# Four of 22 channel pairs of an up projection by seven products of halves, and weight sums by adding transfers

## The chip, the cores and the metric

The kernel runs on one core of one Trainium2 chip. The metric is the device time of one execution in microseconds (us). Five engines work side by side, each through its own queue in order: PE (matmuls), DVE (VectorE), ACT (ScalarE), POOL (GpSimd) and SP, which issues transfers (DMAs). On-chip memory is SBUF (128 partitions) and PSUM, where matmuls accumulate; PSUM is used here as banks of 128 x 512 f32.

## The reference, cut to what matters

One encoder block over 512 tokens of 1024 channels. The change concerns the channel mixer at its end:

```python
h2 = rmsnorm(x, norm2_w[l])
u = dwconv_centered(h2 @ ffn_up[l], ffn_conv_w[l], ffn_conv_b[l])   # 1024 -> 2 x 2816, width 3 over tokens
gate, val = jnp.split(u, 2, axis=-1)
x = x + (jax.nn.silu(gate) * val) @ ffn_down[l]                     # 2816 -> 1024
return rmsnorm(x, final_norm_w)
```

Everything is float32. The kernel keeps that precision by splitting each operand into a high part (rounded to the PE's reduced format, fp32r) and a low part (the rest), and by three matmuls for each product: high x high, high x low, low x high (`mm3`, L370 to L373).

## The kernel before

**The up projection** (534 to 776 us). The 5632 columns of ffn_up are taken as 22 channel pairs: for pair c the 128 gate columns c and the 128 value columns c. Each of the 44 jobs (`job`) loads a weight tile wr_up of 128 x 8 x 128, ACT copies it to the high part wh_up, POOL subtracts to get the low part wl_up in two operations of 512 elements a partition, and PE makes 8 x 3 matmuls over all 512 tokens into one PSUM bank, ps_up. The rings of buffers set how far ahead this may run: three wr, two wh, two wl, three banks of the ring "pp". Then `conv3` applies the width-3 convolution from PSUM: ACT makes the centre tap with the bias (L1674), DVE the two side taps (L1680), each reading the bank and adding into an SBUF tile c3. ACT applies SiLU to the gate, and DVE multiplies gate by value into a (L1701). The first job (c = 0) is done in two halves of 256 tokens.

**The down product** already uses seven products of halves instead of eight: it is cut into halves of tokens, of its 22 inner blocks (11 and 11) and of output columns (one step of the Strassen scheme, in Winograd's form). Its left operands (sums and differences of a's blocks, cut into high and low parts "as" by L1630 on ACT and L1634 on DVE) are partly made in the up stage: parts 1 and 7 for each c below 11, L1643's combinations for each c from 11. Its right operands are four sums of blocks of ffn_down. `t_unit` makes them in the up stage, eleven times: SP loads two row blocks of ffn_down into the tile tp (L1657), POOL makes four differences in place (L1665), and SP writes each to DRAM, t_scr (L1667). The down product reads them back as wr_dn.

**What sets the order.** A small list scheduler, `Planner`, holds every operation with its engine, an assumed cost, the names it reads and writes, and a key; it fixes one order for each engine before the program runs. Keys come in three ranks, FEED (weights) before EVICT (emptying PSUM) before the rest, and within a rank by the unit's number u. On the chip each engine goes through its list in order and waits only for what an instruction needs.

## Time and profile before

| | |
|---|---|
| runs of the kernel before | 891.85, 890.25, 890.43 us; median 890.43 |
| the profiled execution | 890.88 us, of which the span is 889.2 us |
| PE's mean granted clock | 0.996 of full |
| PE's busy share of the span | 98% |
| up projection on PE | first matmul 534.6 us, last 776.1 us |
| down product and final norm | to 889.2 us |

Times in rows of the profile are microseconds from the span's start, unless marked ns. A row of the groups gives line, engine, operation, tiles written <- read, shape, count | busy us, mean ns of one | idle time of the engine just before, and what ended it. A tile's or a line's row gives min/median/max ns and the first and the last start. PEld is the loading of weights into PE, which overlaps matmuls.

### The profile page before, as it was taken

To read this page: it belongs to the slowest core of one execution; us is meant where nothing else is said; L and a number is where in the kernel's file an instruction comes from. 1 tells how busy PE (TensorE), PEld (TensorE's weight loads), DVE (VectorE), ACT (ScalarE), POOL (GpSimd) and SP (SyncE) were. 2 spreads that over 40 slices of the span, in tenths; PEclk is the share of its full clock that TensorE was granted. 3 is DMA by queue.
4 is the path that set the end of the run, shared out by engine and by line. 5 is a ranking of instruction groups with operands and counts; after the bars stand their busy time and mean duration, and the time that the engine had idled before them with its cause. 6 is when DMAs were issued, how large, how long until landed. Compare 5 with 4: busy or idle time off the path is not lost.

```text
span 889.2 us, 14088 instructions
## 1 busy us (share of the span) xinstructions
PE 874.7 (98%) x5178; PEld 737.1 (83%) x5178; DVE 549.0 (62%) x980; ACT 461.0 (52%) x791; POOL 497.9 (56%) x447
## 2 busy tenths in 40 slices
PE   8999999999999999999999999999999999999996
PEld 7888888798878887988788888888888888888885
DVE  4757685357795976554434244656655554569995
ACT  6689533418868334335854334444443333456664
POOL 3444555125455553253668706778787764567663
PEclk9999999999999999999999999999999999999999
DMA  7365449324255376112898606567666753266553
GB/s 207 99 204 131 130 118 188 86 60 119 64 163 154 108 168 107 31 60 73 275 306 270 190 1 231 187 213 225 233 202 203 244 173 101 97 211 181 186 178 133
DMA packets 176265, 140.20 MB, mean 158 GB/s; under 512 B 32110, under 2 KB 143547, under 8 KB 176196
## 3 DMA queue, kind: packets, MB, share of 16 engines
q1 hardware_dynamic: 167300, 137.20, 51.1%
q10 hardware_dynamic: 8896, 2.10, 1.6%
q8 instruction: 41, 0.67, 0.3%
q14 instruction: 28, 0.23, 0.1%
HBM read 114.08 MB, written 25.20 MB: 157 GB/s over the span
## 4 chain that ended last, share of the span: by engine, by line
PE 92%; DVE 3%; ACT 2%; DMA 2%; issue 1%; SPq 0%; DVEq 0%; ACTq 0%
PE ps_up L372 9%; PE ps_up L371 9%; PE ps_up L373 9%; PE dn L373 3%; PE dn L371 3%; PE dn L372 3%; PE ps_k L371 2%; PE pw L1139 2%; PE o L1176 2%; PE ps_k L373 2%; PE ps_gp L371 2%; PE ps_k L372 2%; PE ps_wo L373 2%; PE ps_wo L372 2%; PE ps_wo L371 2%; PE ps_gp L372 2%
## 5 line engine op out<-in xcount | busy, mean ns | idle before, releaser
L396 POOL TENSOR_TENSOR wl_up<-wr_up,wh_up 128x512 fp32r<-128x512 f32 x88 | 115.2, 1330 | 50.1 <-ACT wh_up L392 47.9
L372 PE MATMUL ps_up<-h_lo,wh_up 128*128 128x512 f32 (+1 forms) x368 | 139.9, 380 | 0.3 <-DVE h_lo L541 0.3
L371 PE MATMUL ps_up<-h_hi,wh_up 128*128 128x512 f32 (+1 forms) x368 | 140.0, 380 | 0.0
L373 PE MATMUL ps_up<-h_hi,wl_up 128*128 128x512 f32 (+1 forms) x368 | 139.8, 380 | 0.0
L1680 DVE SCALAR_TENSOR_TENSOR c<-ps_up,fw,c 128x511 f32<-128x511 f32 x88 | 66.0, 750 | 99.3 <-ACT c L1674 97.5
L1665 POOL TENSOR_TENSOR tp<-tp 128x512 f32<-128x512 f32 x44 | 59.9, 1362 | 43.4 <-DMA tp<-in_ffn_down_dram 38.5
L1868 POOL TENSOR_TENSOR w_dn<-wr_dn,w_dn 128x512 fp32r<-128x512 f32 x44 | 65.6, 1504 | 29.0 <-ACT w_dn L1865 27.5
L372 PEld LDWEIGHTS ps_up<-h_lo,wh_up 128*128 128x128 f32 x368 | 69.1, 188 | 13.5 <-DVE h_lo L541 0.5
L371 PEld LDWEIGHTS ps_up<-h_hi,wh_up 128*128 128x128 f32 x368 | 69.1, 188 | 13.3
L373 PEld LDWEIGHTS ps_up<-h_hi,wl_up 128*128 128x128 f32 x368 | 69.1, 188 | 13.2
L392 ACT CAST wh_up<-wr_up 128x1024 fp32r<-128x1024 f32 x44 | 46.2, 1051 | 62.1 <-issue 22.3
L1865 ACT CAST w_dn<-wr_dn 128x512 fp32r<-128x512 f32 x69 | 42.4, 621 | 29.5 <-PE dn L373 21.1
L372 PE MATMUL dn<-w_dn,as 128*128 128x512 f32 x141 | 54.2, 385 | 0.0
L371 PE MATMUL dn<-w_dn,as 128*128 128x512 f32 x141 | 54.2, 384 | 0.0
L373 PE MATMUL dn<-w_dn,as 128*128 128x512 f32 x141 | 54.2, 384 | 0.0
L1634 DVE TENSOR_TENSOR as<-a,as 128x512 fp32r<-128x512 f32 (+1 forms) x41 | 41.8, 1044 | 0.1
L1630 ACT CAST as<-a 128x512 fp32r<-128x512 f32 (+1 forms) x41 | 21.5, 534 | 32.5 <-DVE a L1701 28.9
L396 POOL TENSOR_TENSOR wl_k<-wr_k,wh_k 128x512 fp32r<-128x512 f32 x16 | 20.3, 1288 | 31.6 <-ACT wh_k L392 22.4
L396 POOL TENSOR_TENSOR wl_v<-wr_v,wh_v 128x512 fp32r<-128x512 f32 x16 | 20.4, 1294 | 27.5 <-ACT wh_v L392 27.5
L1674 ACT ACTIVATE c<-ps_up,fw 128x512 f32<-128x512 f32 x44 | 33.9, 770 | 0.0
L396 POOL TENSOR_TENSOR wl_z<-wr_z,wh_z 128x512 fp32r<-128x512 f32 x16 | 20.3, 1292 | 23.5 <-ACT wh_z L392 19.9
L396 POOL TENSOR_TENSOR wl_gp<-wr_gp,wh_gp 128x512 fp32r<-128x512 f32 x16 | 21.5, 1360 | 19.6 <-ACT wh_gp L392 18.0
(361 smaller groups left out, 2435.8 us busy)
## 6 DMA issues: line engine op xcount, KB each, us to landing
wr_up<-in_ffn_up_dram SPq DMA_DIRECT2D x44, 512.0 KB, 3.9
tp<-in_ffn_down_dram SPq DMA_DIRECT2D x22, 512.0 KB, 5.3
t_scr<-tp SPq DMA_DIRECT2D x44, 256.0 KB, 2.5
wr_dn<-t_scr SPq DMA_DIRECT2D x20, 512.0 KB, 3.8
wr_dn<-in_ffn_down_dram SPq DMA_DIRECT2D x15, 512.0 KB, 3.6
x<-in_x_dram SPq DMA_DIRECT2D x8, 512.0 KB, 6.1
wr_k<-in_w_in_dram SPq DMA_DIRECT2D x8, 512.0 KB, 5.9
wr_z<-in_w_in_dram SPq DMA_DIRECT2D x8, 512.0 KB, 3.9
```

The costliest lines, as they stand in the source:

```text
L371: pe.matmul(ps, ahi, bhi, start=first, stop=False)
L372: pe.matmul(ps, ahi, blo, start=False, stop=False)
L373: pe.matmul(ps, alo, bhi, start=False, stop=last)
L392: act.copy(b["hi"], b["raw"])
L396: pool.tensor_tensor(out=b["lo"][:, sl], in0=b["raw"][:, sl], in1=f32(b["hi"][:, sl]), op=ALU.subtract)
L1630: act.copy(sets[p][:, i : i + n, 0, :], src())
L1634: dve.tensor_tensor(out=w[:, :, 1, :], in0=src(), in1=f32(w[:, :, 0, :]), op=ALU.subtract)
L1665: G(cp(512), lambda o=o, x=x, y=y: pool.tensor_tensor(out=w(*o), in0=w(*x), in1=w(*y), op=ALU.subtract), r=[n(*x), n(*y)], w=[n(*o)], key=u)
L1674: act.activation(b[j], box["ps"], AF.Identity, scale=fw[:, 1, ci : ci + 1], bias=fw[:, 3, ci : ci + 1])
L1680: dve.scalar_tensor_tensor(out=y[:, lo:hi], in0=box["ps"][:, lo + sh : hi + sh], scalar=fw[:, k, ci : ci + 1], in1=y[:, lo:hi], op0=ALU.mu ...
L1865: act.copy(b["w"][:, 0, :], raw["t"][:, j, :])
L1868: eng.tensor_tensor(out=b["w"][:, 1, :], in0=raw["t"][:, j, :], in1=f32(b["w"][:, 0, :]), op=ALU.subtract)
```

## The change

It has two parts and what follows from them.

**Seven products for pairs 3, 5, 7 and 9** (`SEVEN`). For such a pair the product of [gate columns | value columns] with h2 is cut into halves of the 1024 input channels (1, 2) and halves of the tokens; the two column blocks are the second cut of the weight. Seven products of 4 x 3 matmuls with 256 columns take the place of two of 8 x 3 with 512. Four sums of h2's quarters are made once (`h_sums`, into the tile h_raw) and cut into high and low parts (as_x0, as_x1). Each pair's weights need four sums of weight halves, two on POOL and two on DVE, and seven splits (wq): high parts on ACT, low parts five in seven on POOL and two on DVE. The seven PSUM results are combined on DVE into an SBUF tile u of 128 x 1024 by one copy on ACT and seven additions, and the convolution reads u in place of PSUM.

**The four weight sums of the down product** are made without SBUF: `right_sums` issues, from POOL's queue, a transfer of up to 4 x 128 rows from ffn_down (or from a finished t_scr) to t_scr, and then a transfer that adds a second block to it. There are 12 such twos, 24 transfers, spread over pairs 1 to 17. Since they add where POOL subtracted, the signs of some blocks change: the left combinations and five of the additions into the residual are subtractions now.

As the buffers of the ring "as" hold h2's sums until pair 9, parts 1 and 7 of the down product's left operands are made later, two blocks at a time, from pair 9 on (`left_early`, `left_sums`).

The core of the diff:

```diff
-        "r4": 4, "nm": 1, "x4": 3, "qe": 4, "ext": 1, "x1": 1, "x2": 1, "xs": 2, "pw": 1, "pwr": 1, "cv3": 4, "sq2": 1, "as": 2, "tp": 1, "dhl": 3,
+        "r4": 4, "nm": 1, "x4": 3, "qe": 4, "ext": 1, "x1": 1, "x2": 1, "xs": 2, "pw": 1, "pwr": 1, "cv3": 4, "sq2": 1, "as": 2, "tp": 2, "dhl": 3,
+    SEVEN = (3, 5, 7, 9)
+    VLO = (0, 3)
+    MINUS = ((0, 1, 1), (1, 1, 1), (1, 1, 7), (0, 1, 6), (1, 1, 6))
-    def t_unit(i, u):
...
+    def right_sums(j, k0, n, key, after):
...
+        first, second = {0: ((0, 0), (0, 1)), 1: (0, (1, 1)), 2: ((0, 1), (1, 1)), 3: (1, (1, 0))}[j]
+        kept = isinstance(first, int)
+        move = lambda src, **kw: pool.dma_start(flat_(j), src, **kw)
+        add("pool", 1.2, lambda: move(flat_(first) if kept else block(*first)), name(first) if kept else [], name(j),
+            key, None, 256.0 * n, after=after, land=12.0)
+        add("pool", 1.2, lambda: move(block(*second), accum_op=ALU.add), [], name(j), key, None, 256.0 * n, land=12.0)
-    def conv3(box, pp, ci, b, j, u):
+    def conv3(src, srcn, ci, b, j, u):
...
-                out=y[:, lo:hi], in0=box["ps"][:, lo + sh : hi + sh], scalar=fw[:, k, ci : ci + 1],
+                out=y[:, lo:hi], in0=src()[:, lo + sh : hi + sh], scalar=fw[:, k, ci : ci + 1],
+    def h_sums(u):
...
+        for i, o in enumerate(((0, 0), (0, 1), (1, 1), (1, 0))):
+            part(i, *o)
+        comb(4, (0, 0), (0, 0), (0, 1), ALU.subtract)
+        comb(5, (0, 1), (0, 1), (1, 1), ALU.subtract)
+        comb(6, (1, 1), (1, 1), (0, 0), ALU.add)
+        comb(7, (1, 0), (1, 0), (1, 1), ALU.subtract)
+        for i, o in enumerate(((0, 0), (1, 1), (0, 1), (1, 0))):
+            keep(i, o)
+    def seven_weights(c, u):
...
+        split(a11, k)
+        split(a12, k + 1)
+        plus(q1, a21, a22, QV[0], k + 2)
+        plus(q2, q1, a11, QV[1], k + 3)
+        split(q2, k + 4)
+        plus(a21, a21, a11, QV[2], k + 5)
+        split(a21, k + 6)
+        split(q1, k + 7)
+        plus(a12, a12, q2, QV[3], k + 8)
+        split(a12, k + 9)
+        split(a22, k + 10)
+    def seven_up(c, b):
...
+        for i in range(7):
+            tag = ("ds", "pp")[turns["l"] % 2]
...
+                mm3(p["ps"], wt_[:, 0, k, :], wt_[:, 1, k, :], *xs[i][0](k), k == 0, k == 3)
...
+            act.copy(at(1, 0), box[0][0]["ps"])
+        step((0, 0), 1, (1, 0), ALU.add)
+        step((1, 1), 2, (1, 0), ALU.subtract)
+        step((1, 0), 3, (1, 1), ALU.add)
+        step((0, 1), 4, (1, 1), ALU.subtract)
+        step((1, 1), 4, (1, 0), ALU.subtract, swap=True)
+        step((0, 1), 5, (0, 1), ALU.add)
+        step((1, 0), 6, (1, 0), ALU.add)
+    TURNS = {n: 1 for n in (1, 2, 4, 5, 7, 8, 10, 11, 13, 14, 16, 17)}
+    QV = (0, 1, 0, 1)
+    SLOTS = ("dhl", "whi", "wlo", "dhl", "whi", "wlo", "dhl")
+        if c in SEVEN:
+            u = seven_up(c, b)
+        if pos == 0:
+            h_sums(u + 1000)
+        for _ in range(TURNS.get(pos, 0)):
+            right_sums(*turn_.pop(0), 5000, [f"cv3:{c}"])
-        if c % 2 == 0:
-            t_unit(c // 2, u + 60)
```

What this does to the order is seen at three places. Names in the rows: c3_N is the convolution's tile of chunk N (gate chunks 0 to 21, value chunks 22 + c), ps_upC_J the PSUM result J of pair C, wr_uJ_C and wq_C_I the raw and the split weights of a seven-product pair, u_C its combined result; numbers at a name's end only tell buffers apart.

Place one, DVE, from the moment at which h2 is complete. Before:

```order
L1680 SCALAR_TENSOR_TENSOR c3_0_5538<-ps_up0_0_5408,fw_130,c3_0_5538 128x511 x2
L1680 SCALAR_TENSOR_TENSOR c3_22_5566<-ps_up0_1_5448,fw_130,c3_22_5566 128x511 x2
L1701 TENSOR_TENSOR a_0_5591<-c3_0_5538,c3_22_5566 128x512
L1643 TENSOR_TENSOR c3_22_5566<-a_0_5591 128x256
L1634 TENSOR_TENSOR as_1_5599<-a_0_5591,as_1_5599 128x256
L1634 TENSOR_TENSOR as_7_5604<-c3_22_5566,as_7_5604 128x256
L1680 SCALAR_TENSOR_TENSOR c3_1_5620<-ps_up1_0_5561,fw_130,c3_1_5620 128x511 x2
```

And now:

```order
L1704 TENSOR_TENSOR h_raw_5491<-h2_hi_4724,h2_lo_4725 128x4x256 x3
L1680 SCALAR_TENSOR_TENSOR c3_0_5531<-ps_up0_0_5408,fw_130,c3_0_5531 128x511 x2
L1704 TENSOR_TENSOR h_raw_5491<-h2_hi_4724,h2_lo_4725 128x4x256
L1680 SCALAR_TENSOR_TENSOR c3_22_5557<-ps_up0_1_5445,fw_130,c3_22_5557 128x511 x2
L1904 TENSOR_TENSOR a_0_5583<-c3_0_5531,c3_22_5557 128x512
L1711 TENSOR_TENSOR h_raw_5491<-h_raw_5491 128x4x256 x3
L1680 SCALAR_TENSOR_TENSOR c3_1_5603<-ps_up1_0_5552,fw_130,c3_1_5603 128x511 x2
L1711 TENSOR_TENSOR h_raw_5491<-h_raw_5491 128x4x256
```

Seven passes over quarters of h2, 1024 elements each, have come between the taps, with an eighth behind pair 1's first; the three operations on the left operands are gone from here.

Place two, DVE, what follows up to the additions of pair 3. Before, behind pair 1's product:

```order
L1643 TENSOR_TENSOR c3_23_5661<-a_0_5591 128x256
L1634 TENSOR_TENSOR as_1_5599<-a_0_5591,as_1_5599 128x256
L1634 TENSOR_TENSOR as_7_5604<-c3_23_5661,as_7_5604 128x256
L1680 SCALAR_TENSOR_TENSOR c3_2_5707<-ps_up2_0_5651,fw_130,c3_2_5707 128x511 x2
L1680 SCALAR_TENSOR_TENSOR c3_24_5747<-ps_up2_1_5696,fw_130,c3_24_5747 128x511 x2
```

And now:

```order
L1726 TENSOR_TENSOR as_x0_5610<-h_raw_5491,as_x0_5610 128x4x256 x2
L1680 SCALAR_TENSOR_TENSOR c3_23_5653<-ps_up1_1_5592,fw_130,c3_23_5653 128x511 x2
L1904 TENSOR_TENSOR a_0_5583<-c3_1_5603,c3_23_5653 128x512
L1760 TENSOR_TENSOR h_raw_5491<-h_raw_5491,wr_u0_3_5581 128x512
L1726 TENSOR_TENSOR as_x1_5634<-h_raw_5491,as_x1_5634 128x4x256
L1781 TENSOR_TENSOR wq_3_2_5699<-h_raw_5491,wq_3_2_5699 128x512
L1760 TENSOR_TENSOR wr_u0_3_5581<-wr_u0_3_5581,h_raw_5491 128x512
L1781 TENSOR_TENSOR wq_3_6_5710<-wr_u1_3_5631,wq_3_6_5710 128x512
L1680 SCALAR_TENSOR_TENSOR c3_2_5692<-ps_up2_0_5639,fw_130,c3_2_5692 128x511 x2
L1726 TENSOR_TENSOR as_x1_5634<-h_raw_5491,as_x1_5634 128x4x256
L1680 SCALAR_TENSOR_TENSOR c3_24_5747<-ps_up2_1_5681,fw_130,c3_24_5747 128x511 x2
L1840 TENSOR_TENSOR u_3_5760<-ps_up3_1_5749,u_3_5760 128x256
```

The taps of pair 2 (c3_2, c3_24), which empty its two banks, stand behind the low parts of h2's sums and behind pair 3's weights.

Place three, POOL, from pair 2's gate weights on. Before:

```order
L396 TENSOR_TENSOR wl_up2_0_5614<-wr_up2_0_5238,wh_up2_0_5613 128x512 x2
L1665 TENSOR_TENSOR tp_1_5555<-tp_1_5555 128x512
L396 TENSOR_TENSOR wl_up2_1_5656<-wr_up2_1_5572,wh_up2_1_5655 128x512 x2
L396 TENSOR_TENSOR wl_up3_0_5701<-wr_up3_0_5593,wh_up3_0_5700 128x512 x2
L1665 TENSOR_TENSOR tp_2_5688<-tp_2_5688 128x512 x2
L396 TENSOR_TENSOR wl_up3_1_5740<-wr_up3_1_5649,wh_up3_1_5739 128x512 x2
```

And now:

```order
L400 TENSOR_TENSOR wl_up2_0_5597<-wr_up2_0_5238,wh_up2_0_5596 128x512 x2
L1781 TENSOR_TENSOR wq_3_0_5619<-wr_u0_3_5581,wq_3_0_5619 128x512
L400 TENSOR_TENSOR wl_up2_1_5644<-wr_up2_1_5563,wh_up2_1_5643 128x512 x2
L1760 TENSOR_TENSOR h_raw_5491<-wr_u1_3_5631 128x512
L1760 TENSOR_TENSOR wr_u1_3_5631<-wr_u1_3_5631,wr_u0_3_5581 128x512
L1781 TENSOR_TENSOR wq_3_1_5685<-wr_u0_3_5581,wq_3_1_5685 128x512
L1664 DMA t_scr_104<-in_ffn_down_dram 512x512
L1781 TENSOR_TENSOR wq_3_3_5704<-wr_u1_3_5631,wq_3_3_5704 128x512
L1781 TENSOR_TENSOR wq_3_4_5729<-h_raw_5491,wq_3_4_5729 128x512
L1781 TENSOR_TENSOR wq_3_5_5740<-wr_u0_3_5581,wq_3_5_5740 128x512
L400 TENSOR_TENSOR wl_up4_0_5789<-wr_up4_0_5674,wh_up4_0_5788 128x512 x2
L1664 DMA t_scr_104<-in_ffn_down_dram 512x512
```

The differences in tp have gone from POOL; pair 3 brings five low parts and two sums in place of four low parts, and between them stands the first of the 24 transfers; the second follows pair 4's gate weights.

200 lines of the change are left out of this document (158 added, 42 removed).

## The prediction, made before the changed kernel ran

> **What bounds the kernel now.** First the head of the page: the span, the busy time of the engines, PE in 40 slices, and the chain of work that ended last.
>
> ```profile
> span 889.2 us, 14088 instructions
> PE 874.7 (98%) x5178; PEld 737.1 (83%) x5178; DVE 549.0 (62%) x980; ACT 461.0 (52%) x791; POOL 497.9 (56%) x447
> PE   8999999999999999999999999999999999999996
> PE 92%; DVE 3%; ACT 2%; DMA 2%; issue 1%; SPq 0%; DVEq 0%; ACTq 0%
> ```
>
> PE is full in all but the first and the last slice and holds 92% of the chain, so the time is what PE is given to do plus whatever it waits for. The second view sums PE's waits; the third is the stretch from the second pair of the up projection to the down product (busy us of each engine with the number of instructions, clock, DMA share, GB/s); the fourth, all instructions on the up projection's PSUM tile (min/median/max ns, first and last start).
>
> ```profile
> PE ps_up L372 <- DVE h_lo L541: 0.3, 1, 0.3
> ...
> 547.00:777.00 230.00, 230.00 (x1020) 190.53 (x1019) 130.84 (x163) 98.09 (x135) 167.13 (x127) 1.00 0.59 192
> ...
> L371 PE MATMUL ps_up<-h_hi,wh_up x368: 280/389/403, 534.6 to 775.6; 128*128 128x512 f32 x168, 128*128 128x256 f32 x16
> L373 PE MATMUL ps_up<-h_hi,wl_up x368: 278/389/397, 534.8 to 776.1; 128*128 128x512 f32 x168, 128*128 128x256 f32 x16
> ```
>
> In the up projection PE waits once, 0.3 us, at its start; after 547 us it is busy for all 230 us, while POOL has 167 and DVE 131. A matmul taken off PE here is worth its full step; a wait put on PE costs its full length.
>
> **The step of a matmul.** A row's 389 ns overlaps the next instruction, so the price is the distance between starts.
>
> ```profile
> 543.06 0.28 PE L371 MATMUL ps_up<-h_hi,wh_up 128*128 128x256 f32 x1
> ...
> 547.62 0.28 PE L373 MATMUL ps_up<-h_hi,wl_up 128*128 128x256 f32 x1
> 547.74 0.40 PE L371 MATMUL ps_up<-h_hi,wh_up 128*128 128x512 f32 x1
> ...
> L371 PEld LDWEIGHTS ps_up<-h_hi,wh_up 128*128 128x128 f32 x368 | 69.1, 188 | 13.3
> ```
>
> Between the first two rows lie 38 steps of a 256-column matmul: 4.56 us, 0.120 us each. From 547.74 to the last start at 776.1 lie 1007 steps of 512 columns (42 products of 24): 0.2268 us each. The half-width step is therefore 53% of the full one, not 50%. That the 188 ns of a weight load would set the pace of half-width matmuls (84 x 0.188 = 15.8 us a pair, slower) is refuted by the same rows, which load a new weight for each.
>
> **PE's gain.** A pair is now 2 x 8 x 3 = 48 steps of 512: 10.89 us. By seven products it is 7 x 4 x 3 = 84 steps of 256: 10.08 us. The gain is 0.81 us a pair, **3.24 us** for four. The down product keeps its seven products and its matmuls; only its additions into the residual change sign and operand order.
>
> **What the other engines get.** POOL loses 44 subtractions and 16 low parts (four pairs), and gets 20 low parts and 8 sums of halves of the same size, and 24 transfers to issue. DVE gets 12 passes over a quarter of h2, 8 sums, 8 low parts, and 28 additions out of PSUM. ACT gets 32 copies of small tiles for 8 of larger ones; it is busy 98 of 230 us and I count it as hidden. Their prices:
>
> ```profile
> L396 POOL TENSOR_TENSOR wl_up<-wr_up,wh_up x84: 1283/1294/1815, 546.1 to 767.8; 128x512 fp32r<-128x512 f32 x84
> L1665 POOL TENSOR_TENSOR tp<-tp x40: 1283/1296/1742, 551.5 to 717.9; 128x512 f32<-128x512 f32 x40
> L1680 DVE SCALAR_TENSOR_TENSOR c<-ps_up,fw,c x88: 737/750/753, 546.8 to 779.0; 128x511 f32<-128x511 f32 x88
> L1634 DVE TENSOR_TENSOR as<-a,as x11: 410/426/1521, 554.7 to 662.2; 128x256 fp32r<-128x256 f32 x11
> L1701 DVE TENSOR_TENSOR a<-c,c x22: 691/888/1845, 551.6 to 779.7; 128x512 f32<-128x512 f32 x22
> L522 DVE SCALAR_TENSOR_TENSOR sq<-x,nst_b,n2b 128x1024 f32<-128x1024 f32 x4 | 5.1, 1286 | 0.1
> ```
>
> POOL's account falls: 60 operations go, 28 come, so 32 x 1.295 = 41 us less, against 24 issues whose length no row shows; over the stage that is room, not gain, since PE does not wait for POOL now. DVE's grows: a pass over 1024 elements is about 1.25 us (0.41 at 256, 0.69 at 512, so 0.28 per further 256; 1.286 is the nearest row), 12 of them 15 us; 16 x 0.69 = 11 us; 28 additions of 256 elements at about 0.42 = 12 us. These 38 us would take DVE from 131 to 169 of 230 us: enough on the average. What decides is where it is needed at once, and that is ahead of the first of the four pairs.
>
> **DVE and POOL shut each other out.** In the two rows of DVE and the one of POOL (three operations), DVE's 256-element operation, 0.41 us when alone, takes 1.40 and 1.52 us beside POOL's.
>
> ```profile
> 553.37 1.40 DVE L1643 TENSOR_TENSOR c<-a 128x256 f32<-128x256 f32 x1
> 554.70 1.52 DVE L1634 TENSOR_TENSOR as<-a,as 128x256 fp32r<-128x256 f32 x1
> ...
> 551.50 4.43 POOL L1665 TENSOR_TENSOR tp<-tp 128x512 f32<-128x512 f32 x3
> ```
>
> L1680, with one input in PSUM, never does (737 to 753 ns in 88). The Trainium skill, page "SBUF — State Buffer", section "Who interferes with whom", has the rule: a DVE instruction with two SBUF inputs contends with a GpSimd instruction that reads SBUF, one with at most one does not. By that rule the trace agrees, and the 16 taps of the four pairs, which now read SBUF, fall under it too.
>
> The groups of DVE from 547 to 777 us give the mean of such a wait (mean ns is the second number):
>
> ```profile
> L1701 DVE TENSOR_TENSOR a<-c,c 128x512 f32<-128x512 f32 x21 | 21.2, 1010 | 1.1 <-ACT c L1703 0.4
> ...
> L1634 DVE TENSOR_TENSOR as<-a,as 128x256 fp32r<-128x256 f32 x11 | 10.1, 919 | 0.1
> ...
> L1634 DVE TENSOR_TENSOR as<-c,as 128x256 fp32r<-128x256 f32 x11 | 7.8, 705 | 0.7 <-ACT as L1630 0.4
> ```
>
> Over the shortest ones (691, 410, 410) that is 0.32, 0.51 and 0.30 us: 0.4 an operation.
>
> **The first seven-product pair.** h2 is complete when DVE's two h_lo operations end:
>
> ```profile
> 541.26 1.29 DVE L541 TENSOR_TENSOR h_lo<-pt_b,h_hi 128x512 fp32r<-128x512 f32 x2 [2.72 <-ACT h_hi L537]
> ```
>
> at 542.55. Pair 3 starts on PE after 96 steps from 547.74, at 569.5. Its fourth product (36 steps of 0.120 later, 573.8) takes the PSUM bank of pair 2's gate, since the ring "pp" has three; so pair 2's two taps on that bank must be done by then. By DVE's order (places one and two) there stand before their end: 11 passes of 1024 (13.8 us), 10 taps (7.5), 2 products gate x value (0.89 each, 1.8), 4 operations of 512 (2.8): 25.9 us, up to 568.4 if nothing waits. That leaves 5.4 us for the waits of 17 operations with two SBUF inputs. At 0.4 each they are 6.8 and PE stands 1.4 us. The upper end: POOL has 14 operations (18 us) in these 31, and where both engines queue they alternate, as in the rows at 551 to 556, so that most of the 17 wait up to 1.0 us; going through the two orders in turn I find some 8.5 us of waits and a stop of 3.1; ten waits of 1.0 would give 4.6. The lower end is none, if the operations fall into POOL's gaps. I take the middle of 1.4 and 3.1, **2.3 us**. The next three pairs need no passes over h2: their DVE work ahead of a product is two sums and two low parts, their weights are read a pair ahead, and I count them at nothing; if that cover is gone, it is the second rival. An addition out of PSUM is on the path only if late; 28 of them are priced above.
>
> **The transfers.** 24 issues stand in POOL's queue between low parts that PE needs, and an adding one waits there for the copy it adds to. Nearest rows:
>
> ```profile
> tp<-in_ffn_down_dram SPq DMA_DIRECT2D x22, 512.0 KB, 5.3
> wr_dn<-t_scr SPq DMA_DIRECT2D x20, 512.0 KB, 3.8
> ```
>
> A transfer of 1 MB, DRAM to DRAM, is at least 3.8 us and, at twice the slower row, 10.6; with a second operand to read up to twice that, 21. Each issue may cost POOL from nothing to about one operation (1.3 us). Between a copy and its adding transfer POOL's order leaves about 9 us at the tightest place: the second copy stands behind pair 4's gate weights, about 11 us into pair 3, its adding transfer behind pair 5's sums, about 20 us in (pair 4's gate product frees their slot at 15.5, then three POOL operations). Elsewhere it is 13 to 18. Behind the tightest one some 4 us are left until PE needs the next low part. I take 7 us, by the row it is nearest to (the load of the same data), and no cost. SP loses 66 DMAs and POOL-dependent waits; nothing waited for them but POOL.
>
> **Sum.** The profiled execution took 890.88 us: 890.88 - 3.24 + 2.3 = 889.94. It lies 0.45 above the median of the runs shown, 890.43, so against that **889.5 us**, 0.1% faster, with 888.1 to 891.7 as this case's own range (a stop of 0.9 to 4.5). The measurement tells about 0.2% (1.8 us) from no change.
>
> **Rivals.** *Nothing stops* (0.35): the passes over h2 fit the gaps, PE stays full, 890.43 - 3.24 = 887.2. For it: 5.4 us of room. Against: POOL fills 17.4 of 21 us in that stretch now, and more afterwards.
> *DVE and POOL are full in pairs 5, 7 and 9 too* (0.13): over two pairs (10.89 + 10.08 = 21.0 us of PE) POOL has 11 operations, 14.2 us, and DVE 10 with two SBUF inputs, 7.5 us (two products, four of 512, four taps): 21.7 us that exclude each other. It decides where handing over between the two saves nothing. Against: at 551 to 556 us POOL's three and two of DVE's (0.69 and 0.41 alone) took 4.43 us and not 5.0, so a hand-over saves 0.2 to 0.3. If it saves nothing, each of the three pairs is late by 1 to 1.5 us: 889.5 + 3.7 = **893.2**, slower.
> *POOL is held by an adding transfer* (0.12): it decides from a landing over 13 us; at 18 us the tightest place loses 5: **894.5**. The Trainium skill, page "Collectives: The Full Stack", section "The bandwidth ceiling: the fold count and why AG ≠ RS ≠ AR", says that a reducing transfer reads two sources and ran at about half a copy's rate there (1.93). No run here shows it; by it 7 us would be about 13, just at that point.
>
> ```profile
> 547.00:568.00 21.00, 21.00 (x98) 17.47 (x97) 14.42 (x18) 11.22 (x16) 17.43 (x14) 1.00 0.72 236
> ```
>
> **How the numbers follow.** Forecast 0.40, rivals 0.35, 0.13, 0.12. Faster by over 0.2% (below 888.65) is the first rival and the low edge of the forecast: 0.38. Within 0.2%: 0.37. Slower (above 892.2): 0.25. The range 886.8 to 893.6 holds the forecast, the first rival with 0.4 us below, and most of the second; it leaves out the third.
>
> **What would show it.** Right: PE's rows step 0.120 us through pairs 3, 5, 7 and 9, and one gap of about 2 us lies before pair 3's fourth product, released by DVE (a tap of pair 2). No gap at all: the first rival. Gaps of about 1 us in each of pairs 5 to 9, released by DVE or POOL: the second. POOL idle ahead of an adding transfer, with PE waiting for a low part: the third. A gap in the down product, or more than 3.5 us saved, would say that I have missed a part of the change.

## The result, and the profile after

| | before | changed |
|---|---|---|
| median of 5 runs each | 890.8 us (890.25 to 892.2) | 905.94 us (904.32 to 906.27) |
| ratio, with its 95% interval | | 1.0164 (1.0152 to 1.0176) |
| profiled execution; its span | 890.88; 889.2 us | 906.27; 904.4 us |

The change makes the kernel 1.6% slower; 889.5 us was predicted, with 893.6 as the upper end. First the head of the changed kernel's page: the busy time of the engines, PE and its granted clock in 40 slices, and the chain that ended last.

```profile
PE 880.8 (97%) x5322; PEld 746.9 (83%) x5322; DVE 584.9 (65%) x1011; ACT 470.6 (52%) x809; POOL 483.2 (53%) x439
...
PE   8999999999999999999999999898899999999997
...
PEclk9999999999999999999999999998999999999999
...
PE 78%; DVE 11%; DMA 4%; ACT 3%; issue 2%; POOL 1%; DVEq 0%; SPq 0%; ACTq 0%; POOLq 0%
```

PE held 92% of the chain before and holds 78% now; what it lost went to DVE (3 to 11%) and to DMA (2 to 4%). Apart from the first and the last, PE's slices 26, 28 and 29 are no longer full, and slice 28 of its clock; all of them lie in the up projection. How long that stage is can be read from one line's rows; this is the same line as L373 of before (first and last start 534.8 and 776.1, 241.3 us apart):

```profile
L377 PE MATMUL ps_up<-h_hi,wl_up x304: 278/389/497, 537.3 to 790.2; 128*128 128x512 f32 x136, 128*128 128x256 f32 x16
```

252.9 us: the stage that was to become 3.2 us shorter is 11.6 longer. Of the 15.2 us between the spans the rest is 2.5 us ahead of the stage (taken for chance, since a second profile of before below moves by 1.7) and 1.1 us behind it. The windows of the changed kernel tell where (busy us of PE, PEld, DVE, ACT, POOL with the number of instructions, clock, DMA share, GB/s):

```profile
570.00:600.00 30.00, 27.20 (x176) 24.79 (x175) 26.81 (x32) 14.69 (x25) 24.76 (x20) 1.00 0.73 184
600.00:625.00 25.00, 22.57 (x135) 20.25 (x135) 16.86 (x20) 9.66 (x15) 15.77 (x13) 0.94 0.73 190
625.00:650.00 25.00, 23.08 (x121) 20.64 (x120) 15.31 (x20) 7.06 (x12) 14.80 (x13) 0.85 0.90 205
...
700.00:793.00 93.00, 93.00 (x412) 77.02 (x411) 41.59 (x54) 37.44 (x49) 51.23 (x45) 1.00 0.76 197
```

The first three hold most of the stops in pairs 3, 7 and 9; from 700 us on, where the transfers still run beside pairs of eight products, PE is full. In two of the windows the granted clock is below 1 as well. The waits of PE in the stage, and what moved on the queues (issues with KB and median us to landing; the last line is the landing of the loads wr_u of the seven-product pairs, with a load of weights before the change ahead of it):

```profile
PE ps_up L375 <- ACT wq L1778: 3.0, 3, 1.7
PE ps_up L375 <- DVE c L1680: 2.8, 1, 2.8
PE ps_up L377 <- DVE wq L1781: 1.8, 2, 1.1
PE ps_up L377 <- POOL wq L1781: 0.8, 1, 0.8
```

```profile
wr_up<-in_ffn_up_dram SPq DMA_DIRECT2D x36, 512.0 KB, 4.4
t_scr<-in_ffn_down_dram POOLq DMA_DIRECT2D x12, 1024.0 KB, 10.7
...
wr_up<-in_ffn_up_dram SPq DMA_DIRECT2D x44, 512.0 KB, 3.9
...
DMA to landing us min/median/max: 5.0/10.7/16.3
```

Only the wait of 2.8 us, for DVE's tap, is the predicted one. The others are for split weights (wq), and the loads behind them are late. The last line knows the landing of only two of the eight loads, 5.0 and 16.3 us, and its 10.7 is their middle. The semaphore updates in the trace (sixteen for each transfer, of which the last is the landing) give all eight: 3.8 to 16.3 us, median 8.0, and 8.8 or more for the four of pairs 7 and 9, where a load of weights took 3.9 before. The chain of waits through pairs 7 and 9:

```profile
601.73 9.95 DMA wr_u<-in_ffn_up_dram
611.70 0.62 ACT wq L1778
612.33 0.72 ACT c L1674
613.08 1.51 DVE c L1680
614.61 4.38 DVE c L1680
...
627.71 16.35 DMA wr_u<-in_ffn_up_dram
644.08 0.63 ACT wq L1778
```

A load of pair 7 takes 9.95 us. ACT stands in its order at the split of that load, and behind the split stands the centre tap of pair 5, so DVE's taps start late too. They then meet POOL, which is at work on the same load:

```profile
613.08 5.90 DVE L1680 SCALAR_TENSOR_TENSOR c<-u,fw,c 128x511 f32<-128x511 f32 x2 [0.21 <-ACT c L1674]
...
614.63 1.29 POOL L1760 TENSOR_TENSOR h_raw<-wr_u 128x512 f32<-128x512 f32 x1
615.88 1.29 POOL L1781 TENSOR_TENSOR wq<-wr_u,wq 128x512 fp32r<-128x512 f32 x1
617.12 1.29 POOL L1760 TENSOR_TENSOR wr_u<-wr_u,wr_u 128x512 f32<-128x512 f32 x1
```

Two taps out of SBUF, 0.75 us each out of PSUM, take 5.90 us (one alone is 4.38 in the chain); the second ends 0.6 us after POOL's third operation. Only then come DVE's sums for pair 7, and PE has stood since 619.8. Pair 9 has it shorter: a load of 16.35 us, and PE waits for the split. Last, PE itself at two of the stops (of one matmul: start, us, and in brackets the idle time before and what ended it):

```profile
576.17 0.28 PE L377 MATMUL ps_up<-as_x,wq 128*128 128x256 f32 x1
579.25 0.36 PE L375 MATMUL ps_up<-as_x,wq 128*128 128x256 f32 x1 [2.80 <-DVE c L1680]
579.45 0.28 PE L376 MATMUL ps_up<-as_x,wq 128*128 128x256 f32 x1
579.57 0.28 PE L377 MATMUL ps_up<-as_x,wq 128*128 128x256 f32 x1
...
621.73 0.39 PE L375 MATMUL ps_up<-as_x,wq 128*128 128x256 f32 x1 [1.74 <-ACT wq L1778]
...
622.95 0.58 PE L377 MATMUL ps_up<-as_x,wq 128*128 128x256 f32 x1 [0.70 <-DVE wq L1781]
623.33 0.41 PE L375 MATMUL ps_up<-as_x,wq 128*128 128x256 f32 x1
623.54 0.41 PE L376 MATMUL ps_up<-as_x,wq 128*128 128x256 f32 x1
```

After pair 3's stop the matmuls follow, from the second step on, at 0.12 us again. After pair 7's they follow at 0.213 us for 26 steps, 2.4 us lost after the wait is over; the window of these steps has the granted clock at 0.50:

```profile
623.20:628.60 5.40, 5.40 (x26) 5.40 (x27) 3.94 (x6) 3.16 (x6) 5.40 (x5) 0.50 0.02 7
```

So there are two kinds of loss. A **stop** is the distance between two starts of the trace less the step; a **slow step** is one of 0.213 in place of 0.120. Summed over the stage the stops are 10.6 us (2.9 in pair 3, 7.7 in pairs 7, 9 and 10) and the slow steps 4.0 (43 of them), and 241.3 - 3.2 + 10.6 + 4.0 = 252.7 of the 252.9 us.

### The profile page after: what moved, and what is told of

Same layout as the page of the kernel before. It is cut to its first block, busy times and chain, and to the rows that moved or that the text cites. A ratio compares the mean times of both kernels' runs of the same rounds, so it can differ in the third digit from the quotient of the medians.

```text
span 904.4 us, 14307 instructions
## 1 busy us (share of the span) xinstructions
PE 880.8 (97%) x5322; PEld 746.9 (83%) x5322; DVE 584.9 (65%) x1011; ACT 470.6 (52%) x809; POOL 483.2 (53%) x439
## 4 chain that ended last, share of the span: by engine, by line
PE 78%; DVE 11%; DMA 4%; ACT 3%; issue 2%; POOL 1%; DVEq 0%; SPq 0%; ACTq 0%; POOLq 0%
PE ps_up L377 6%; PE ps_up L375 6%; PE ps_up L376 6%; DMA wr_u<-in_ffn_up_dram 3%; DVE as L1640 2%; PE ps_k L375 2%; PE pw L1143 2%; PE o L1180 2%; PE ps_k L377 2%; PE ps_gp L375 2%; PE ps_k L376 2%; PE ps_wo L377 2%; PE ps_wo L375 2%; PE ps_wo L376 2%; PE ps_gp L376 2%
## 5 line engine op out<-in xcount | busy, mean ns | idle before, releaser
L400 POOL TENSOR_TENSOR wl_up<-wr_up,wh_up 128x512 fp32r<-128x512 f32 x72 | 99.7, 1410 | 102.6 <-ACT wh_up L396 102.5
L376 PE MATMUL ps_up<-h_lo,wh_up 128*128 128x512 f32 (+1 forms) x304 | 115.0, 378 | 0.3 <-DVE h_lo L545 0.3
L377 PE MATMUL ps_up<-h_hi,wl_up 128*128 128x512 f32 (+1 forms) x304 | 115.0, 378 | 0.2 <-POOL wl_up L400 0.2
L375 PE MATMUL ps_up<-h_hi,wh_up 128*128 128x512 f32 (+1 forms) x304 | 115.1, 379 | 0.0
L1680 DVE SCALAR_TENSOR_TENSOR c<-ps_up,fw,c 128x511 f32<-128x511 f32 x72 | 53.9, 749 | 59.2 <-ACT c L1674 58.0
L2073 POOL TENSOR_TENSOR w_dn<-wr_dn,w_dn 128x512 fp32r<-128x512 f32 x44 | 66.6, 1533 | 27.5 <-ACT w_dn L2070 24.9
L377 PEld LDWEIGHTS ps_up<-h_hi,wl_up 128*128 128x128 f32 x304 | 57.2, 188 | 11.3 <-POOL wl_up L400 0.6
L376 PEld LDWEIGHTS ps_up<-h_lo,wh_up 128*128 128x128 f32 x304 | 57.2, 188 | 11.0 <-DVE h_lo L545 0.5
L375 PEld LDWEIGHTS ps_up<-h_hi,wh_up 128*128 128x128 f32 x304 | 57.2, 188 | 10.6
L1781 POOL TENSOR_TENSOR wq<-wr_u,wq 128x512 fp32r<-128x512 f32 x16 | 23.4, 1463 | 17.7 <-ACT wq L1778 17.7
L376 PEld LDWEIGHTS dn<-w_dn,as 128*128 128x128 f32 x141 | 26.5, 188 | 7.4 <-DVE w_dn L2073 2.1
L400 POOL TENSOR_TENSOR wl_gd<-wr_gd,wh_gd 128x512 fp32r<-128x512 f32 x16 | 20.4, 1297 | 20.0 <-ACT wh_gd L396 20.0
## 6 DMA issues: line engine op xcount, KB each, us to landing
t_scr<-in_ffn_down_dram POOLq DMA_DIRECT2D x12, 1024.0 KB, 10.7
```

Of the source, the lines that this page charges most:

```text
L375: pe.matmul(ps, ahi, bhi, start=first, stop=False)
L376: pe.matmul(ps, ahi, blo, start=False, stop=False)
L377: pe.matmul(ps, alo, bhi, start=False, stop=last)
L400: pool.tensor_tensor(out=b["lo"][:, sl], in0=b["raw"][:, sl], in1=f32(b["hi"][:, sl]), op=ALU.subtract)
L1680: dve.scalar_tensor_tensor(out=y[:, lo:hi], in0=src()[:, lo + sh : hi + sh], scalar=fw[:, k, ci : ci + 1], in1=y[:, lo:hi], op0=ALU.mult, ...
L1781: eng.tensor_tensor(out=b["w"][:, 1, :], in0=x[0](), in1=f32(b["w"][:, 0, :]), op=ALU.subtract)
```

## The experiments

The theory after the result, A: the transfers delay the loads, a pair of seven products cannot bear late loads, and a pair of eight can. Against it: B, that DVE and POOL are full in such pairs whatever the transfers do; C, that POOL is held by the issues or by waiting for a copy; D, that the transfers take something other than the loads' time. The table gives for each kernel the median of its runs, that of before on the same chip, the stage's length as above (nominal is 241.3 less 0.81 for each pair by seven products), the median and the longest landing of the eight loads wr_u (six in seven_6) by the trace's semaphore updates, the stops, and the slow steps. The last four columns are of one profiled execution each. Executions of one kernel differ by some us (small_transfers from 894.75 to 899.06, sp_copies from 892.93 to 897.95), so a difference of 1 or 2 us of stops between two kernels is weak. The expectations below speak of the landing that the view gives, the middle of two of the eight loads: 10.7 us in the changed kernel, 7.2 in copies, 5.4 in small_transfers.

| kernel | median us | before | stage us | landing: median; longest | stops | slow steps |
|---|---|---|---|---|---|---|
| changed | 905.94 | 890.8 | 252.9 | 8.0; 16.3 | 10.6 | 4.0 |
| transfers_alone | 893.83 | 892.03 | 241.2 | none | 0 | 0 |
| seven_alone | 894.85 | 892.03 | 244.0 | 3.8; 5.1 | 3.2 | 2.8 |
| transfers_late | 907.74 | 892.03 | 242.9 | 3.8; 4.6 | 3.2 | 1.6 |
| copies | 901.83 | 892.03 | 247.6 | 6.0; 10.7 | 7.7 | 1.7 |
| own_tile | 904.8 | 891.49 | 253.9 | 6.7; 12.4 | 10.7 | 5.1 |
| early3 | 912.57 | 891.49 | 242.9 | 3.8; 4.9 | 3.3 | 1.6 |
| early4 | 909.19 | 891.49 | 242.0 | 3.8; 5.1 | 2.3 | 1.7 |
| small_transfers | 897.07 | 891.14 | 246.4 | 4.8; 5.9 | 6.5 | 1.8 |
| sp_copies | 895.47 | 891.14 | 244.4 | 5.2; 9.0 | 5.9 | 0.4 |
| order_alone | 895.55 (one run) | 891.35 | 244.6 | 5.0; 5.6 | 4.0 | 2.5 |
| order_other | 906.49 | 891.35 | 254.7 | 5.9; 10.0 | 12.5 | 4.0 |
| half_rows | 895.37 (one run) | 891.35 | 244.7 | 5.6; 10.4 | 4.9 | 1.8 |
| seven_6 | 887.79 | 891.35 | 239.1 | 3.8; 4.0 | 0 | 0.1 |

### One part alone

```diff
-    SEVEN = (3, 5, 7, 9)
+    SEVEN = ()                       # transfers_alone
-    TURNS = {n: 1 for n in (1, 2, 4, 5, 7, 8, 10, 11, 13, 14, 16, 17)}
+    TURNS = {}                       # seven_alone
```

> The second part of the change alone: all 22 pairs by eight products, the weight sums of the down product by adding transfers at the same pairs as in the changed kernel. Theory A (the transfers delay the loads of weights, 512 KB in 10 us and more in place of 3.9, and a seven-product pair, which holds two of the three raw tiles at once, cannot bear it): the loads of wr_up are late here too, but pairs of eight products bear it, as pairs 10 to 17 of the changed kernel did with 0.4 us of stops: 891 to 893 us. Theory B (DVE and POOL are full in the seven-product pairs, whatever the transfers do): no such pair, so 890 to 891. Theory C (POOL is held by the issues and the adding transfers, for every kind of pair): 895 to 905.

> The first part alone: pairs 3, 5, 7 and 9 by seven products, no transfers; the down product reads unsummed blocks of ffn_down in place of the four sums, so the sums are left out and the output is not the reference's. Theory A: the stop of 3 us before pair 3's fourth product stays, the other three pairs run without a stop, loads of weights land in about 4 us: 890.8 - 3.2 + 3.0 = 890.6, within 1.5. Theory B: the stops of 2.9 and 4.0 us in pairs 7 and 9 and the slower steps after them stay: 900 to 904. Theory C: 888 to 891.

With the transfers alone the stage is as long as before, to 0.1 us:

```profile
L377 PE MATMUL ps_up<-h_hi,wl_up x368: 278/389/389, 539.5 to 780.7; 128*128 128x512 f32 x168, 128*128 128x256 f32 x16
```

Its median is 0.2% above before's (ratio 1.002, 1.0005 to 1.0035); in the profiled execution no part of that lies in this stage. With seven products alone, pairs 5, 7 and 9 run without a stop and the loads land in 3.8 us, 5.1 at most, as A says and B denies. The stage is still 2.7 us longer than before, where A has it 0.2 shorter (whole kernel 1.0021, 1.0006 to 1.0036): the slow steps that A did not know of take 2.8, here behind pair 3's stop.

```profile
574.26 0.28 PE L377 MATMUL ps_up<-as_x,wq 128*128 128x256 f32 x1
577.34 0.55 PE L375 MATMUL ps_up<-as_x,wq 128*128 128x256 f32 x1 [2.80 <-DVE c L1680]
577.69 0.41 PE L376 MATMUL ps_up<-as_x,wq 128*128 128x256 f32 x1
```

Neither part costs in the stage what the two cost together: -0.1 and +2.7 us apart, +11.6 in one kernel.

### The transfers moved away from the seven-product pairs

```diff
+    TURNS = {n: 1 for n in range(10, 22)}        # transfers_late
+    EARLY = ["pp:gp0", "pp:gp4", "pp:p0", "pp:p2", "ds:pw0", "ds:pw2", "pp:po0", "pp:po4", "pp:do0"]
+    TURNS = {n: 1 for n in (11, 13, 15)}         # early3, early4
+    for n in EARLY:
+        right_sums(*turn_.pop(0), 5000, [n])
```

> The whole change with the twelve twos of transfers moved to pairs 10 to 21, behind the last seven-product pair. Theory A: only pair 3's stop stays, and the pairs of eight products bear the transfers: 890.5 to 893. Theory B: as the changed kernel less 1 at most, 903 to 905. Theory C: the loss moves with the transfers, 900 to 905, with stops in pairs 10 to 21.

> The whole change with nine of the twelve twos of transfers moved ahead of the up projection (behind jobs of the stages at 290 to 500 us) and three to pairs 11, 13 and 15; pairs 3, 5, 7 and 9 as before by seven products. Theory A: the up projection takes what it took with seven products alone, 2.8 us more than before the change (pair 3's stop and the half clock after it, less the gain of 3.2), and eight-product jobs bear the transfers: 892 to 896 us. If the earlier stages do not bear them, stops appear there: 896 to 905.

> As the run before, with pairs 4, 6, 8 and 10 by seven products instead of 3, 5, 7 and 9, which gives the twelve passes over h2 one more pair of time (10.9 us). Theory A with pair 3's stop put down to DVE's backlog: no stop at all, the gain of 3.2 us is left, 887 to 890 us, and under the kernel before. If the stop has another cause (the first seven-product pair itself, whatever goes before): a stop of 3 us in pair 4, 892 to 896.

In both kernels that keep pairs 3, 5, 7 and 9 only pair 3's stop is left, and the stage falls from 252.9 to 242.9 us. That part of A is borne out twice. In transfers_late the loads wr_up beside the transfers take up to 13.5 us, and no pair of eight products stops. The times are not borne out. In transfers_late the transfers reach into the down product (from the stage's last start to the end of the span 120.6 us, 113.1 before), where PE waits 4.4 us for a tap and for low parts; what lies behind these waits was not traced, and the profiled execution, at 904.09 us, leaves 3.6 us of the median unexplained. In early3 the transfers lie beside the loads of the stages ahead:

```profile
t_scr<-in_ffn_down_dram POOLq DMA_DIRECT2D x8, 1024.0 KB, 10.6
wr_do<-in_dn_out_dram SPq DMA_DIRECT2D x8, 512.0 KB, 13.6
```

```profile
PE ps_do L375 <- ACT wh_do L396: 8.3, 2, 8.2
```

Again the line for wr_do is the middle of two loads, 6.8 and 20.4 us; the median of all eight is 7.8 us, against 5.1 (6.2 at most) in the kernel before. PE waits 8.2 us at once for what follows from this load, in jobs that know nothing of seven products. So it is the loads that the transfers delay, wherever they are, and "pairs of eight products bear it" holds only where the loads have slack.

In early4 pair 4 has no stop, as A expected with one more pair of time for DVE's passes, but pair 6 has one of 2.0 us, which it did not expect.

### Bytes, addition, issues or order

```diff
-        add("pool", 1.2, lambda: move(block(*second), accum_op=ALU.add), [], name(j), ...
+        add("pool", 1.2, lambda: move(block(*second)), [], name(j), ...             # copies
-        move = lambda src, **kw: pool.dma_start(flat_(j), src, **kw)
+        move = lambda src, **kw: pool.dma_start(flat_(j)[:, 0:32], src[:, 0:32], **kw)    # small_transfers
+        move = lambda src, **kw: pool.dma_start(flat_(j)[:, 0:256], src[:, 0:256], **kw)  # half_rows
+        move = lambda src, **kw: None                                               # order_alone
+        L(256.0 * n, lambda: sp.dma_start(...), ...                                 # sp_copies, both of a two
-        add("pool", 1.2, ..., 256.0 * n, land=12.0)
+        add("pool", 0.0, ..., 0.01, land=12.0)                                      # order_other, both of a two
```

> The whole change with the second transfer of each two as a plain copy in the same place, so the addition is left out and the output is not the reference's. It prices the addition itself. Theory A with the load put down to the addition (it reads two sources): a transfer of 1 MB lands in clearly less than 10.7 us and the time falls to 895 to 900. Theory A with the load put down to the bytes and descriptors, whether they add or not: landing within 15% of 10.7 us and 904 to 906. Theory B: 904 to 906 either way.

> The whole change with 24 transfers at the same places of POOL's queue and with as many rows, but only 32 of 512 columns of each row: 1/16 of the bytes. The down product reads unsummed blocks of ffn_down, so most of the sums are left out and the output is not the reference's. Theory A (bytes of the transfers delay the loads): the up projection, from its first matmul to the first of the down product, takes what it took without transfers, 244.5 us within 1.5, and loads of wr_u land in 4 to 6 us: 891 to 896 us. Theory C (POOL's issues and its waits for the transfers are the cost): 250 to 253 us, 900 to 905.

> The whole change with 24 plain copies from SP's queue in place of POOL's 12 copies and 12 adding transfers, of the same bytes and at the same pairs, the second of each two into a scratch of its own; the addition is left out and the output is not the reference's. It takes POOL's issues and the adding away and keeps the bytes. Theory A: loads of wr_u still land in 6 us or more, and the up projection takes 246 to 250 us, as with copies from POOL's queue (248.1): 895 to 902 us. Theory C: 244.5 us, 891 to 894.

> The changed kernel's order of instructions on every engine, with the 24 transfers left out and nothing in their place (the down product reads unsummed blocks, so the sums are left out and the output is not the reference's). Behind pair 3, PE stood still 0.2 us with seven products alone (where the scheduler, not knowing of transfers, chose another order), 3.3 us with small transfers in the changed order, 8.0 us in the changed kernel. If the order makes the 3.3: 2.5 to 3.5 us of stops behind pair 3 here. If POOL's 24 issues make them: at most 0.5.

> All 24 transfers, copies and adding ones, but planned at no cost and no bytes, so that the order of everything else is that of the kernel with seven products alone. Theory A (late loads make the stops whatever the order): 5 us or more of stops behind pair 3, wr_u landing in 8 us or more, 901 to 906 us. If the changed order is what turns the transfers into stops: under 2.5 us of stops, 893 to 898.

> The changed kernel with 256 of 512 columns of every row in the 24 transfers: half the bytes, as many rows, the addition kept (the down product reads unsummed blocks; the output is not the reference's). Theory A with bytes as the load: wr_u lands in 7 to 9 us, halfway between 5.4 (1/16 of the bytes) and 10.7, and the stops behind pair 3 are 5 to 6.5 us. If it is the number of rows that an adding transfer is cut into: landing near 10 and stops near 8 us.

The order alone is worth 0.8 us of stops behind pair 3 (between the two expectations, near the second), and the transfers in the other order make 9.6: it is not the order that turns them into stops. With plain copies in the same place the stage is 5.3 us shorter, and the transfers land faster:

```profile
t_scr<-in_ffn_down_dram POOLq DMA_DIRECT2D x12, 1024.0 KB, 7.0
```

So the addition is 2.9 of the 7.7 us of stops behind pair 3, and of the slow steps at most 2.3; the kernel stays 2 us above what A expected of it. The rest does not follow one quantity. Half the bytes with the addition kept has the two loads of the view at 7.1 us, as A said, and one of the eight at 10.4, but leaves 1.9 us of stops, not 5 to 6.5. A sixteenth of the bytes leaves 3.5, though its loads take 5.9 at most; its stage and time, 246.4 and 897.07 us, lie just above A's (243 to 246 and 891 to 896) and below C's. And order_alone, the same order without any transfer, has 5.6 at most and leaves 0.8. SP's copies of all the bytes, with no issue on POOL, leave 2.9, and their stage of 244.4 us is what C expected (244.5), not A (246 to 250), while their 895.47 us lies in A's range and not in C's. They slow the loads as well: the second load of pair 7 is issued at 602.15 and lands 9.0 us later, when POOL, which has stood for it, starts at 611.22:

```profile
602.15 0.53 SPq L1753 DMA_DIRECT2D wr_u<-in_ffn_up_dram  x1
...
611.22 1.29 POOL L1762 TENSOR_TENSOR h_raw<-wr_u 128x512 f32<-128x512 f32 x1 [1.39 <-DMA wr_u<-in_ffn_up_dram]
```

Where the longest load took up to 5.9 us, the stops behind pair 3 are 0 to 3.5 us; from 9.0 to 10.7, 1.9 to 9.6; at 12.4 and 16.3 (own_tile, changed), 8.5 and 7.7. Later loads go with longer stops, but they do not set their length. In order_other the 9.6 us go back, at least in part, to single loads, here from the chain of waits at pair 5's:

```profile
583.34 7.62 DMA wr_u<-in_ffn_up_dram
...
591.02 1.62 POOL h_raw L1760
...
592.71 1.63 POOL wr_u L1760
...
598.87 2.27 DVE wr_u L1760
601.14 0.67 DVE c L1680
```

The last row is the tap that frees PE's bank. It has an early input, but stands in DVE's order behind the sums of a load that came late.

C in its first form is out: in the changed kernel POOL waits in this stage for ACT's high parts alone (102.5, 17.7 and 4.9 us), never for a transfer. Another form of it stays open: small_transfers against order_alone (3.5 and 0.8 us of stops, with loads almost equally fast) points to a cost of POOL's 24 issues of 0.5 to 1.4 us that does not come through late loads, and sp_copies against copies (2.9 and 4.8) fits it. With one profile of each, that cost is not separated from chance.

### The loads' place

```diff
-        rn = [f"raw:u{n}{c}" for n in "gv"]
+        rn = [f"raw:ug{c}", f"tp:uv{c}"]
```

(with the tile of the value weights taken from the ring tp.)

> The whole change, with the value weights of the four seven-product pairs in a slot of the ring tp instead of the ring of three raw tiles, so that each pair's second load can be issued earlier by about one job; nothing else is moved. Theory A (a seven-product pair holds two of three raw tiles, so its loads are issued late, and beside the transfers they land too late for pairs 7 and 9): of the 11.4 us that stops and halved clock cost in pairs 7 and 9, at most 4 stay: 896 to 900 us; pair 3's stop stays. Theory D (the transfers take from something else, such as SBUF access of ACT, DVE and POOL, and loads are not the point): 903 to 906.

A fell here in its simple form, and the time is what D expected (903 to 906 us). Counted from the start of the stage, the loads of pairs 7 and 9 land 6 to 9 us earlier than in the changed kernel (the first of pair 7 at 66.7 us in place of 74.4, the first of pair 9 at 97.6 in place of 106.8), yet the stops behind pair 3 are 8.5 us. PE's waits have changed owner:

```profile
PE ps_up L375 <- DVE c L1680: 5.0, 2, 4.6
PE ps_up L375 <- ACT c L1674: 3.1, 1, 3.1
```

A wait for weights became a wait for taps, as in order_other. The chain of waits at pair 7 still begins at a load (7.67 us), but then runs through four taps of DVE that took 6.58 us together, beside POOL's operations, and through the sums of the load that stand ahead of the next taps. So a late load alone does not set the length of a stop, and D, that DVE and POOL take time from each other, is not refuted for what follows it.

### DVE's backlog, and the start of the program

```diff
-    SEVEN = (3, 5, 7, 9)
+    SEVEN = (6, 8, 10)               # seven_6; TURNS = {} as in seven_alone
```

> Seven products alone (no transfers, the sums left out, the output is not the reference's) in pairs 6, 8 and 10. DVE's twelve passes over h2 have 33 us more before they are needed than with pair 3. If the stop of 3 us was this backlog: no stop of over 0.5 us, up projection 241.7 - 2.4 = 239.2 us, 888 to 890 us. If a first seven-product pair stops whatever its place: 3 us in pair 6, 242 us, 891 to 893.

> The kernel before once more, for a second profile. In the changed kernel's profile the up projection starts 2.3 us later than in that of before, all of it from the first 11 us of the program, which the change does not touch. If that is chance, this profile's up projection starts anywhere from 534 to 539 us; if it belongs to the change, at 534.6 within 0.5.

No stop and no slow step: with 33 us more for the passes, three pairs save 2.2 of the 2.43 us, and the time is under before's (ratio 0.996, 0.9945 to 0.9974), with the sums left out. Pair 3's stop was the backlog.

```profile
L377 PE MATMUL ps_up<-h_hi,wl_up x320: 278/389/390, 535.0 to 774.1; 128*128 128x512 f32 x144, 128*128 128x256 f32 x16
```

The kernel before, profiled again, has its stage of 241.2 us start 1.7 us later, so a shift of this size ahead of the stage is chance:

```profile
L373 PE MATMUL ps_up<-h_hi,wl_up x368: 278/389/397, 536.5 to 777.7; 128*128 128x512 f32 x168, 128*128 128x256 f32 x16
```

### The sums in SBUF again

Four complete kernels without adding transfers: `own_sums` loads two row blocks of ffn_down, adds four times and stores, as `t_unit` did.

```diff
+    OWN = (1, 3, 11, 12, 13, 14, 15, 16, 17, 18, 19)    # own_sums4, SEVEN = (4, 6, 8, 10)
+    OWN = (0, 1, 2, 11, 12, 13, 14, 15, 16, 17, 18)     # own_sums5, SEVEN = (5, 7, 9)
+    OWN = (0, 1, 3, 4, 11, 13, 14, 16, 17, 19, 20)      # own_sums6, SEVEN = (6, 8, 10)
+    OWN = (0, 2, 4, 5, 11, 13, 14, 16, 17, 19, 20)      # own_sums6b, SEVEN = (6, 8, 10), two additions on DVE
```

> The first part of the change with the weight sums in SBUF again: no adding transfers; eleven units of two loads, four POOL additions and four stores behind pairs 1, 3 and 11 to 19, and seven products in pairs 4, 6, 8 and 10. Theory A (loads late through the transfers are what costs, and pair 3's stop is DVE's backlog): PE without a stop of over 1 us in pairs 4 to 10, 241.7 - 3.2 = 238.5 us for the up projection, 888 to 890 us, under the kernel before. Theory B (DVE and POOL shut each other out too much as soon as POOL has the sums as well): stops in pairs 4 to 10 or behind 11, 892 to 900.

> As the run before, with three pairs, 5, 7 and 9, by seven products and the units of sums behind pairs 0, 1, 2 and 11 to 18: the gain is 2.4 us in place of 3.2, and DVE's twelve passes have two more pairs of time than in the changed kernel. Theory A: no stop of over 1 us, 239.3 us for the up projection, 888.5 to 890.5. Theory B: stops in pairs 5 to 9, 892 to 900.

> A complete version that may beat both: seven products in pairs 6, 8 and 10, no adding transfers, and the weight sums as units in SBUF (two loads, four POOL additions, four stores) behind pairs 0, 1, 3, 4, 11, 13, 14, 16, 17, 19 and 20, so that none lies in or between seven-product pairs. Theory A: up projection 239 to 241 us, 888 to 890 us in all, under the kernel before. If two units in neighbouring pairs make POOL late with low parts (POOL then has 8 operations of 1.3 us in 10.9 us, and stops of 1 to 2 us stood there with three pairs by seven products and units behind 0, 1, 2 and 11 to 18): 3 to 8 us more, 892 to 898.

> As the run before, with two of the four additions of a unit on DVE instead of POOL and the units behind pairs 0, 2, 4, 5, 11, 13, 14, 16, 17, 19 and 20. If POOL's load is what makes stops there: fewer stops than in the run before, up projection 239 to 241 us, 887.5 to 890. If the two engines shut each other out just as much whichever of them adds: as the run before or slower, DVE's taps late, 890 to 896.

930.35, 903.92, 906.41 and 901.19 us: none is under before, and A's numbers failed in all four. The loads wr_u land in 3.9 to 5.1 us again (medians). In the up projection PE now waits most for POOL's low parts, in all four (3.8 to 5.4 us), here in own_sums5:

```profile
PE ps_up L377 <- POOL wl_up L400: 4.6, 5, 1.9
```

That kernel has its eleven units in eleven pairs, one in each, where before had one in every second. POOL is not only busier: it stands in its order at a sum whose row blocks have not landed, 17.1 us in the stage in own_sums5, 6.5 before. In own_sums4 the greater part of the 39 us lies behind the up projection, where ACT waits for loads of weights and PE for ACT:

```profile
PE dn L375 <- ACT w_dn L2087: 17.0, 2, 14.1
```

No complete kernel here beats the one before.

## Why the prediction was wrong

**The transfers** ("I take 7 us ... and no cost") are the step that failed. The 7 us were right for a copy and low for an addition: in the changed kernel the four copies of 1 MB from ffn_down landed in 6.0 to 7.1 us and the eight adding transfers in 10.2 to 13.4 (median 11.0; in copies, 7.6 in the same eight places). What failed is "no cost". I asked what a transfer does to the engine that issues it, and found 9 to 18 us of room there; POOL indeed never waited for one. I did not ask what it does to the transfers beside it. The longest load of the seven-product pairs went from 5.1 us (seven_alone) to 16.3, and behind pair 3 came 7.7 us of stops and 4.0 of slow steps; with the transfers moved away (transfers_late, early3) only pair 3's stop and the slow steps behind it were left. That the transfers beside these pairs cost this is shown. Late loads stand at the head of the chains of waits in pairs 7 and 9; how much of the cost goes through them, and how much through POOL's issues and through DVE and POOL taking time from each other, stays open (own_tile, small_transfers, sp_copies). The Trainium skill, page "Collectives: The Full Stack", section "The bandwidth ceiling: the fold count and why AG ≠ RS ≠ AR", which I weighed only for POOL, has a reducing collective at about half a copying one's rate (1.93); 11.0 against 7.6 us here is less than that.

**The next three pairs** ("their weights are read a pair ahead, and I count them at nothing") failed with it: the cover was the fast load. With loads of at most 5.1 us the count was right (seven_alone, seven_6). With late ones, ACT and DVE stand in their order at the split and the sums of the late load, and the taps that free PE's banks stand behind them.

**Rival 2**, the two engines shutting each other out in pairs 5, 7 and 9, is not there by itself (no stop in seven_alone), but it seems to lengthen a delay once there is one: the two taps of 5.90 us ran beside POOL's operations. **Rival 3** had a part of the cause, the adding transfer, at the wrong place: POOL waited for none.

**The first pair** was right: one stop before pair 3's fourth product, released by DVE's tap, 3.0 us against 2.3 (0.9 to 4.5), and gone where DVE has more time. **PE's gain** was right too: 0.120 us a step and 2.2 of 2.43 us for three pairs.

**What a stop costs** was a term too small: "a wait put on PE costs its full length" left out the slow steps, 4.0 us in the changed kernel and up to 2.8 for a single stop.

**The down product.** A gap there was to mean that I had missed a part of the change. There is one, 1.7 us for DVE's low part w_dn (L2073), in seven_alone as well. In the row ahead of it DVE has four operations on the left parts. The same four stood there before, of the same size, and took half the time:

```profile
870.93 6.90 DVE L1640 TENSOR_TENSOR as<-a,as 128x512 fp32r<-128x512 f32 x4
...
857.18 3.58 DVE L1634 TENSOR_TENSOR as<-a,as 128x512 fp32r<-128x512 f32 x4
```

The first row is the changed kernel, the second the kernel before. In the changed kernel POOL works without a gap from 866.9 to 878.9 us, and each of DVE's four takes 1.7 us beside it; before, POOL has gaps there. seven_6 has the four operations and no such wait. By these rows the gap comes from a meeting of the two engines, as between L1634 and POOL in the prediction's rows, and not from operations that the change adds there.

## What to carry to other kernels

Price an added transfer by what it does to the transfers that share its time, not only by the engine that issues it: look for the load with the least slack between landing and use, and for what is queued in order behind its first use. Two edits that cost little where they are measured alone (nothing and 2.7 us here) can be dear together (11.6), when one uses the slack that the other needs. And a stop of a full PE can cost more than its length. Last, a median in a view may rest on few of the transfers, here on two of eight.

## What the runs showed of the hardware

*After a stop PE may run at half its clock.* The same stop of 3.0 to 3.1 us before pair 3's fourth product was followed by no slow step in four kernels (changed, copies, sp_copies, order_other), by 14 or 15 in four (transfers_late, early3, small_transfers, half_rows) and by 27 in two (seven_alone, order_alone): nothing, about 3 us, or 5.8 us at 0.213. In early4 a stop of 2.0 us brought 16. The Trainium skill, page "TensorE: Matmul & The Clock Gate", section "Part 1: The HAM clock gate (the "warmup" mystery)", has the clock halved by an idle window of about 3.4 us that runs freely; lengths that come in about such windows, and that differ for one and the same stop, agree with that. Its rule in "HAM oscillation — how this bites in real kernels", that only gaps above about 3.4 us matter, does not agree: stops of 2.0 and 3.1 us did it here.

*Transfers slow the loads that run beside them, from either queue.* The loads wr_u of 512 KB took 3.8 us (median; 5.1 at most) without transfers. They took 5.2 (9.0) beside copies from SP's queue, 6.0 (10.7) beside copies of as many bytes from POOL's, and 8.0 (16.3) where half of POOL's transfers add.
